# Last expert step of a mixture-of-experts layer: four experts of 32 slots side by side in place of two passes of 64 slots

## Chip, core and metric

One core of a Trainium2 chip runs the whole kernel. The metric is the device time of one execution in microseconds (us). The matrix engine, TensorE, is PE in the rows, with its weight loads as PEld; VectorE is DVE, ScalarE is ACT, GpSimd is POOL, and SyncE is SP, which issues nearly all transfers from the device's memory.

## The reference

Two layers, each on 256 tokens of 1024 values in float32. A layer is a token mixer (four kinds of attention, gated and summed), a layer norm, a mixture of 32 experts in 8 groups of 4 with two experts for each token, and a second layer norm. The experts, cut to what matters:

```python
scores = sigmoid(xt @ w_router)                      # 256 x 32
g_sel  = argmax(sum of the two best biased scores of each group)
local  = top_k(biased scores of that group, 2)[1]
e_idx  = g_sel * 4 + local
gate   = scores at e_idx, divided by their sum
# for each expert e and each of its tokens:
hid = silu(xb @ w1[e]) * (xb @ w3[e])                # 1024 -> 256
ys  = hid @ w2[e]                                    # 256 -> 1024
y[token] += ys * gate
```

## The kernel before

The program is one straight list of instructions for each engine; a planner orders those of VectorE, ScalarE, GpSimd and SyncE by program order and dependences, while the order of PE in the expert stage is written out by hand (`manual_schedule`). `issue_after(x)` holds an instruction back until x is issued. PE multiplies float32 in two recorded instructions per matmul; a pair of types, a rounded high part and a remainder in the one-pass type float32r, is used where weights are split (`split`, L406: ScalarE copies the high part, VectorE subtracts).

Experts are handled in pairs: pair p is experts p and p + 16, and shares 64 slots, the first expert's tokens ahead of the second's. An expert stage has eight steps, q = 0 to 7, of two pairs, so four experts. A step (from L1449):

- For s = 0 and 1 (experts p, then p + 16) `head` (L1321) multiplies the gathered tokens with w1 and w3: 8 pieces of the contraction times 2 tiles of 64 columns, 512 wide, the tiles at PSUM rows 0 and 64. `hidden` (L1331) makes silu times product on ScalarE and VectorE, with a mask that keeps the rows of this half.
- `combine` (L1404) adds the outputs of the step before to the accumulators, through the transposed one-hot matrix of `flip_key` (L1386).
- In even steps `gates_of` (L1375) brings the gates to the slots by one matmul for each token block.
- `flip` transposes the hidden tiles, and `tail` (L1350) multiplies with w2: 2 passes, 2 halves of the output, 2 pieces, 2 tiles. ScalarE evicts a half, VectorE makes its remainder.

Expert weights are 1 MB tiles, in an order of SBUF slots (`SLOTS`, 20 of them) that `release` walks on: a tile's transfer starts when PE has used up the tile 20 places earlier. Each step takes 12 tiles, eight of w1 and w3 (`load_head`), then four of w2 (`load_out`). SyncE has eight completion semaphores, so at most eight transfers are outstanding.

Ahead of the first step the router's scores are turned into one-hot rows, ranks (`prk`, L1228), keys (`key`, a token's slot in its pair) and counts (`cn`). The first gather (`gather_first`, L1310) needs `x1l`, a remainder made by three VectorE subtractions (`rest`, L1179). Behind them in VectorE's queue stand the counts and gates (L1264 to L1283) and then the first evictions of the gather (`gathered`, L1294: even pieces on VectorE, odd ones on ScalarE).

Behind the last step the number of tokens of the fullest pair is loaded into a register on every engine (L1483), and a branch (L1581) runs the overflow loop over all pairs if it is over 64. Ahead of the branch stand, for the next layer, its first weight loads (`ahead`), `norm2` (L1525: statistics of the accumulators, power, scaling into R) with NW3 matmuls that keep PE busy, and the first two splits of the next layer's first weight (`pieces`). The next layer begins with transposes of R (L435).

## Time and profile before

| | us |
|---|---|
| median of the runs | 1007.54 |
| lowest and highest of the runs | 1006.2, 1008.17 |
| the profiled execution, its own time | 1012.46 |
| its span, first to last instruction | 1010.5 |
| PE busy in the span | 977.2 |

The profiled execution is a single one and has its own time beside its span. The two expert stages lie at about 281 to 502 us and 778 to 999 us. A row of the timeline gives the start and duration of an instruction or of several merged ones (x count), its engine, source line and operation, what it writes and reads, and in brackets how long the engine stood idle before it and what ended that. A row of a window gives the stretch, its length, then busy time and count of each engine, the granted PE clock as a share of 2.4 GHz, the mean busy share of the 16 DMA engines and what they moved.

### The profile page before, as it was taken

The numbers are of one execution on the slowest core, as the hardware profiler recorded it, in microseconds if no ns is written. First come the engines' busy times: TensorE is split into PE (matmuls) and PEld (weight loads), VectorE is DVE, ScalarE is ACT, GpSimd is POOL, SyncE is SP. The second block draws the span as 40 slices with busy tenths as digits, with TensorE's granted clock in tenths as the row PEclk, the third lists the DMA queues.
The fourth block names the chain that finished last, engine by engine and source line by source line (L and its number), as shares of the span: only waits on it lengthen the run. The fifth ranks groups of instructions, "written<-read, shape, count | busy, mean of one in ns | idle before, by whom it ended". The sixth has DMA issues, their size and how long they took to land. (4 is left out here: it accounts for less than half of the span.)

```text
span 1010.5 us, 16677 instructions
## 1 busy us (share of the span) xinstructions
PE 977.2 (97%) x6391; PEld 693.2 (69%) x6391; DVE 494.8 (49%) x1166; ACT 404.3 (40%) x864; POOL 201.8 (20%) x190
## 2 busy tenths in 40 slices
PE   7999999999989999999999999999999999999995
PEld 7989999999953434343497999989998343433432
DVE  4766777667651122221377666685687222211114
ACT  4756665665421212111164766566553111111111
POOL 5440123022020313000045201141112012130001
PEclk9989999999999999999999999999999999999998
DMA  8785444579779999999895454544996799999982
GB/s 276 246 256 166 131 164 127 167 276 410 265 248 395 383 412 413 413 413 413 300 304 143 130 157 135 164 146 157 336 404 212 291 411 412 413 407 414 413 354 85
DMA packets 121434, 287.09 MB, mean 284 GB/s; under 512 B 10398, under 2 KB 73636, under 8 KB 113668
## 3 DMA queue, kind: packets, MB, share of 16 engines
q1 hardware_dynamic: 119940, 282.48, 76.0%
q0 software_dynamic: 1264, 3.41, 1.4%
q8 instruction: 52, 0.85, 0.3%
q14 instruction: 34, 0.28, 0.1%
q10 hardware_dynamic: 144, 0.07, 0.0%
HBM read 284.55 MB, written 1.38 MB: 283 GB/s over the span
## 5 line engine op out<-in xcount | busy, mean ns | idle before, releaser
L417 DVE TENSOR_TENSOR b<-w,b 128x512 fp32r<-128x512 f32 (+2 forms) x294 | 212.7, 739 | 103.3 <-ACT b L412 98.9
L412 ACT ACTIVATE b<-w 128x512 fp32r<-128x512 f32 (+2 forms) x294 | 179.9, 623 | 131.1 <-PE pj L452 106.5
L450 PE MATMUL pj<-big,b 128*128 128x256 f32 x736 | 215.3, 292 | 0.8 <-DVE a L537 0.5
L452 PE MATMUL pj<-big,b 128*128 128x256 f32 x736 | 210.2, 286 | 1.2 <-DVE b L417 1.2
L451 PE MATMUL pj<-big,b 128*128 128x256 f32 x736 | 210.0, 285 | 0.0
L450 PEld LDWEIGHTS pj<-big,b 128*128 128x128 f32 x736 | 142.9, 194 | 7.6 <-issue 4.6
L452 PEld LDWEIGHTS pj<-big,b 128*128 128x128 f32 x736 | 142.9, 194 | 1.7 <-DVE b L417 1.7
L451 PEld LDWEIGHTS pj<-big,b 128*128 128x128 f32 x736 | 143.2, 195 | 0.1
L1327 PE MATMUL h<-xw,a 128*64 128x512 f32 x496 | 127.6, 600 | 4.0 <-DVE a L1300 4.0
L1327 PE MATMUL h<-w,a 128*64 128x512 f32 x400 | 119.3, 593 | 0.0
L1338 DVE SCALAR_TENSOR_TENSOR th<-th,h 128x256 f32<-128x256 f32 x32 | 13.5, 420 | 184.6 <-ACT th L1337 184.6
L1327 PEld LDWEIGHTS h<-xw,a 128*64 128x64 f32 x496 | 44.1, 139 | 74.3 <-issue 67.8
L1337 ACT ACTIVATE th<-h 128x256 f32<-128x256 f32 x32 | 12.3, 384 | 203.5 <-PE h L1327 203.5
L1362 DVE SCALAR_TENSOR_TENSOR b<-y,gcol,b 128x512 fp32r<-128x512 f32 x30 | 22.5, 751 | 112.7 <-ACT b L1361 112.7
L1368 PE MATMUL y<-w,hT 128*64 128x512 f32 x256 | 71.5, 595 | 1.9 <-ACT hT L1347 1.9
L1327 PEld LDWEIGHTS h<-w,a 128*64 128x64 f32 x400 | 37.6, 137 | 44.9 <-issue 44.3
L1361 ACT ACTIVATE b<-y,gcol 128x512 fp32r<-128x512 f32 x30 | 20.6, 688 | 96.7 <-PE y L1368 96.7
L542 POOL TENSOR_TENSOR R<-R,a 128x512 f32<-128x512 f32 x20 | 35.3, 1778 | 111.8 <-DVE a L537 106.3
L450 PE MATMUL pj<-b,big 128*128 128x256 f32 x192 | 55.9, 291 | 1.5 <-ACT b L412 1.3
L452 PE MATMUL pj<-b,big 128*128 128x256 f32 x192 | 55.0, 287 | 0.1
L451 PE MATMUL pj<-b,big 128*128 128x256 f32 x192 | 54.6, 285 | 0.0
L341 POOL TENSOR_TENSOR rs<-ve,mhalf 128x1 f32<-128x1 f32 (+1 forms) x6 | 4.1, 680 | 221.2 <-DVE mr L1538 160.9
(367 smaller groups left out, 1739.4 us busy)
## 6 DMA issues: line engine op xcount, KB each, us to landing
xw<-in_moe_w SPq DMA_DIRECT2D x124, 512.0 KB, 10.2
w<-in_moe_w SPq DMA_DIRECT2D x100, 512.0 KB, 10.2
w<-in_w_gate SPq DMA_DIRECT2D x32, 1024.0 KB, 5.6
w<-in_moe_w SPq DMA_DIRECT2D x32, 1024.0 KB, 12.9
w<-in_w_in SPq DMA_DIRECT2D x18, 1024.0 KB, 10.7
xw<-in_moe_w SPq DMA_DIRECT2D x18, 1024.0 KB, 13.8
w<-in_w_out SPq DMA_DIRECT2D x8, 1024.0 KB, 5.2
ohl<-in_moe_w SPq DMA_DIRECT2D x12, 512.0 KB, 10.5
```

Of the source, the lines that this page charges most:

```text
L412: act.activation(h, v, AF.Copy)
L417: dve.tensor_sub(lo, v, h.bitcast(F32))
L450: pe.matmul(o, lh, rh, start=start, stop=False, skip_group_check=True)
L451: pe.matmul(o, lh, rl, start=False, stop=False, skip_group_check=True)
L452: return pe.matmul(o, ll, rh, start=False, stop=stop, skip_group_check=True).ins
L542: eng.tensor_tensor(merged[:, c:c + 2, :], merged[:, c:c + 2, :], tc_, op=OP.add)
L1327: pe.matmul(ph[64 * i:64 * i + 64], xs(j, i), a13[i][j], start=(j == 0), stop=(j == 7), skip_group_check=True)
L1337: act.activation(tv, h1, AF.Tanh, scale=0.5)
L1338: dve.scalar_tensor_tensor(tv, tv, 1.0, h1, op0=OP.add, op1=OP.mult)
L1361: act.activation(ys[:, 0, :], py, AF.Copy, scale=gcol)
L1362: dve.scalar_tensor_tensor(ys[:, 1, :], py, gcol, ys[:, 0, :].bitcast(F32), op0=OP.mult, op1=OP.subtract)
L1368: pe.matmul(pys[fh][64 * i:64 * i + 64, :], hTs[s][:, c, 64 * i:64 * i + 64], a2[s][i][c][:, fh * 512:fh * 512 + 512], start=(s == 0 and c ...
```

## The change

The last step (q = 7, `QUADS`) holds four experts at once, each with 32 slots of its own. `quad_keys` moves the keys of its four experts: the second expert of a pair gets slots 33 to 64, and a token whose rank is over 32 gets a key beyond the step. `prk` no longer counts the first expert ahead of the second for these pairs (`PAIRED`). `head4` runs one pass of 8 pieces times 4 tiles of 32 columns, `tail` one pass with 4 tiles of 32; there is one `hidden` and one `flip`. The loads of this step come first halves first. A count above 32 in this step sends the rest of these tokens to the overflow loop.

Beside it: the first gather's evictions alternate by pairs of pieces, and gates and counts come behind them; `gates_of` multiplies high part and remainder side by side in float32r and adds them on VectorE; the register loads come behind step 5; in layer 0 the next layer's first two splits come between the last two evictions, the statistics behind them, the branch ahead of the rest of `norm2`, and NW3 is 7 instead of 12. The overflow loop takes the new forms; small scratch arrays move into an existing tile.

```diff
+QUADS = (NQ - 1,)
-NW3 = 12
+NW3 = 7
+PAIRED = slice(2 if 0 in QUADS else 0, NP - 2 if NQ - 1 in QUADS else NP)
...
-                    h, lo = pieces[j] if j < len(pieces) else split(w[j // 4][:, j % 4, 0:n], n, after=xt_ins if j < 4 else None)
+                    h, lo = pieces[j] if j < len(pieces) else split(w[j // 4][:, j % 4, 0:n], n, after=(norm_ins[1] if l else xt_ins) if j < 4 else None)
...
-                    loads += [partial(load_head, q, s, h) for h in range(4)]
+                    if q not in QUADS:
+                        loads += [partial(load_head, q, s, h) for h in range(4)]
+                if q in QUADS:
+                    loads += [partial(load_head, q, s, h) for h0 in (0, 2) for h in (h0, h0 + 1) for s in range(2)]
...
-                pe.matmul(prk[:, :, NP:], oneb, osel[:, tb, None, 0:NP].to_broadcast([128, 2, NP]), start=False, stop=False,
-                          skip_group_check=True)
+                pe.matmul(prk[:, :, NP + PAIRED.start:NP + PAIRED.stop], oneb,
+                          osel[:, tb, None, PAIRED].to_broadcast([128, 2, PAIRED.stop - PAIRED.start]), start=False,
+                          stop=False, skip_group_check=True)
...
+            def quad_keys(q):
+                ps_ = slice(2 * q, 2 * q + 2)
+                kq = key.rearrange("p t (i e) -> p t i e", i=2)[:, :, :, ps_]
+                up = tB[:, 8 * q:8 * q + 8].rearrange("p (t i e) -> p t i e", t=2, i=2)
+                for i, most in enumerate((32.5, 0.5)):
+                    dve.tensor_scalar(up[:, :, i], kq[:, :, i], most, 32.0, op0=OP.is_gt, op1=OP.mult)
+                dve.tensor_add(kq, kq, up)
+                return dve.tensor_add(keyP[:, :, ps_], kq[:, :, 0], kq[:, :, 1]).ins
...
+            if NQ - 1 in QUADS:
+                with tc.issue_after(made):
+                    made = quad_keys(NQ - 1)
             with tc.issue_after(made):
                 for tb, js in ((0, JH[1]), (1, JH[0]), (1, JH[1])):
                     made = rest(dve, tb, js)
...
+            def gates_and_counts():
+                counted = dve.tensor_add(cs, cn[:, 0:NP], cn[:, NP:]).ins
+                with tc.issue_after(counted):
+                    for q in QUADS:
+                        cq = cs[:, 2 * q:2 * q + 2]
+                        dve.tensor_tensor(cq, cn[:, 2 * q:2 * q + 2], cn[:, NP + 2 * q:NP + 2 * q + 2], op=OP.max)
+                        dve.tensor_scalar(cq, cq, 32.0, None, op0=OP.add)
+                    ...
+                    dve.tensor_copy(grs[:, :, :, 0], grP)
+                    dve.tensor_sub(grs[:, :, :, 1], grP, grs[:, :, :, 0].bitcast(F32))
+                    dve.tensor_reduce(cmax, cs, axis=AX.X, op=OP.max)
+                    return dve.tensor_copy(cmi, cmax).ins
...
-                            gathered(xg, j - 1, pxs[j - 1])
-                            gathered(xg, j, pxs[j])
+                            done = [gathered(xg, k, pxs[k], j % 4 == 1) for k in (j - 1, j)][1]
+                return done.ins
...
+            def head4(xs, a13):
+                ph = op.tile([128, 2, 256], F32, name="h")
+                for j in range(8):
+                    for t in range(4):
+                        pe.matmul(ph[32 * t:32 * t + 32], xs(j, t), a13[t][j], start=(j == 0), stop=(j == 7),
+                                  skip_group_check=True, tile_position=(0, 32 * t))
+                return ph
...
-                            for i in range(2):
-                                pe.matmul(pys[fh][64 * i:64 * i + 64, :], hTs[s][:, c, 64 * i:64 * i + 64],
-                                          a2[s][i][c][:, fh * 512:fh * 512 + 512], start=(s == 0 and c == 0),
-                                          stop=(s == len(hTs) - 1 and c == 1), skip_group_check=True)
-                        if s == len(hTs) - 1:
-                            evac(fh)
+                            for r0, n, a2 in tiles:
+                                pe.matmul(pys[fh][r0:r0 + n, :], hT[:, c, r0:r0 + n], a2[c][:, fh * 512:fh * 512 + 512],
+                                          start=(s == 0 and c == 0), stop=(end and c == 1), skip_group_check=True,
+                                          tile_position=(0, r0) if n == 32 else None)
+                        if end:
+                            with tc.issue_after(between()) if fh and between else ExitStack():
+                                evac(fh)
...
-                gp = op.tile([128, 2], F32, name="y")
+                gp = op.tile([128, 2, 2], F32, name="y")
                 for tb in range(2):
-                    pe.matmul(gp, oh[:, tb, :].bitcast(F32), g[:, tb, :], start=(tb == 0), stop=(tb == 1))
+                    pe.matmul(gp, oh[:, tb, :], g[:, tb], start=(tb == 0), stop=(tb == 1))
...
-                    dve.tensor_copy(gcol[H], gp[H, i:i + 1])
+                    dve.tensor_reduce(gcol[H], gp[H, i], axis=AX.X, op=OP.add)
...
+            def next_pieces():
+                pieces.extend(split(ahead[0][0][:, i, :], 416, after=lows[-1]) for i in range(2))
+                return last_split[0]
...
+                    if q == 5:
+                        counts, (cnt_max,) = nc.values_load_multi_w_load_instructions(cmi[0:1, 0:1], min_val=0, max_val=S + 32)
...
+                    if final and l + 1 < layers:
+                        next_slots = list(mixer_slots(l + 1))
+                        ahead = [slot(next_slots[0])]
...
-            norm_ins = norm2(lastc)
+            with ExitStack() if last else tc.issue_after(last_split[1]):
+                stats()
             if not last:
-                pieces = [split(ahead[0][0][:, i, :], 416, after=norm_ins[i]) for i in range(2)]
-            with tc.If(cnt_max > W):
-                with tc.For_i(0, (cnt_max - 1) // W, 1):
-                    dve.tensor_scalar(key, key, float(-W), None, op0=OP.add)
-                    with tc.For_i(0, NP, 1) as pi:
-                        overflow(pi)
-                norm2()
+                with tc.If(cnt_max > W):
+                    rest_of_overflow()
+                norm_ins = norm2(lastc)
+            else:
+                norm2(lastc)
+                with tc.If(cnt_max > W):
+                    rest_of_overflow()
+                    norm2()
```

## Rows read from the trace of the kernel before

**Rows 1.** Page, busy time of each engine, share of the span, instructions.

```profile
PE 977.2 (97%) x6391; PEld 693.2 (69%) x6391; DVE 494.8 (49%) x1166; ACT 404.3 (40%) x864; POOL 201.8 (20%) x190
```

**Rows 2.** Windows over both expert stages; the last columns: PEclk, DMA share, GB/s.

```profile
293.00:468.00 175.00, 172.45 (x842) 73.42 (x840) 36.06 (x81) 27.33 (x56) 23.51 (x19) 0.99 1.02 403
793.00:968.00 175.00, 172.45 (x850) 73.02 (x847) 36.06 (x81) 27.33 (x56) 23.50 (x19) 1.00 1.02 409
```

**Rows 3.** Chain of waits, last steps, layer 1; the third: the timeline.

```profile
964.11 0.61 PE y L1379 x4
...
965.52 7.09 PE y L1368 x32
...
965.53 0.64 PE L1368 MATMUL y<-R,hT 128*64 128x512 f32 x1
...
972.61 13.73 PE h L1327 x64
...
986.34 2.05 PE acc L1412 x8
...
989.52 7.09 PE y L1368 x32
```

**Rows 4.** Timeline: last step of layer 0, then the first eviction in layer 1.

```profile
474.68 10.89 PE L1327 MATMUL h<-xw,a 128*64 128x512 f32 x49
...
491.75 7.09 PE L1368 MATMUL y<-w,hT 128*64 128x512 f32 x32 [0.31 <-ACT hT L1347]
...
497.17 0.69 ACT L1361 ACTIVATE b<-y,gcol 128x512 fp32r<-128x512 f32 x1 [5.20 <-PE y L1368]
...
994.94 0.69 ACT L1361 ACTIVATE b<-y,gcol 128x512 fp32r<-128x512 f32 x1 [5.20 <-PE y L1368]
```

**Rows 5.** Issue, landing: last tile and next weight (layer 0), last tile (layer 1).

```profile
L1015 SPq DMA_DIRECT2D w<-in_moe_w x1: 328/328/328, 473.2 to 473.2; - x1
DMA to landing us min/median/max: 15.1/15.1/15.1
...
L318 SPq DMA_DIRECT2D w<-in_w_in x1: 383/383/383, 474.5 to 474.5; - x1
DMA to landing us min/median/max: 16.0/16.0/16.0
...
L1015 SPq DMA_DIRECT2D w<-in_moe_w x1: 328/328/328, 969.1 to 969.1; - x1
DMA to landing us min/median/max: 14.9/14.9/14.9
```

**Rows 6.** Timeline at the stage start, layer 1; 290.61 is of layer 0.

```profile
290.61 0.33 SPq L1015 DMA_DIRECT2D xw<-in_moe_w  x1
...
777.56 0.19 DVE L1243 TENSOR_TENSOR keyP<-key 128x32 f32<-128x32 f32 x1
...
778.46 3.20 DVE L1180 TENSOR_TENSOR big<-X,big 128x512 fp32r<-128x512 f32 x3
...
782.45 1.72 DVE L1270 TENSOR_SCALAR gr<-gr,gsum 128x32 f32<-128x32 f32 x2
...
784.67 5.81 PE L1327 MATMUL h<-xw,a 128*64 128x512 f32 x18 [2.00 <-DVE a L1300]
...
790.05 0.33 SPq L1015 DMA_DIRECT2D xw<-in_moe_w  x1
```

**Rows 7.** Windows at the stage's start, with the granted clock (PEclk).

```profile
303.30:306.60 3.30, 3.30 (x10) 1.02 (x11) 0.51 (x2) 0.38 (x1) 0.00 (x0) 0.52 1.04 421
...
784.70:788.20 3.50, 3.50 (x10) 1.33 (x12) 1.38 (x4) 2.17 (x5) 0.00 (x0) 0.51 0.37 154
788.20:790.00 1.80, 1.80 (x12) 0.80 (x10) 0.00 (x0) 0.00 (x0) 0.00 (x0) 1.00 0.00 0
```

**Rows 8.** Timeline at the boundary of the layers: a split, the first transpose.

```profile
502.69 0.54 DVE L417 TENSOR_TENSOR b<-w,b 128x416 fp32r<-128x416 f32 x1
...
507.16 0.41 PE L435 MATMUL pj<-K,R 128*128 128x128 f32 x2 [0.30 <-PEq L1581]
```

More of the change, by code (lines that the diff above doesn't have):

```diff
@@ L1348, in flip, with pair_tiles, tail @@
                 return hT
-            def tail(hTs, a2, gcol, out, final=None):
+            lows = []
+            pieces = []
+            def pair_tiles(a2):
+                return [(0, 64, a2[0]), (64, 64, a2[1])]
+            def tail(passes, gcol, out, final=None, between=None):
                 pys = [op.tile([128, 512], F32, name="y") for _ in range(2)]
@@ L1452, in build @@
                     ths = []
-                    for s in range(2):
+                    if q in QUADS:
+                        a13q = [a13s.pop((q, s)) for s in range(2)]
+                        ph = head4(lambda j, t: xgs[b][:, j, o + 32 * t:o + 32 * t + 32],
+                                   [a13q[t % 2][t // 2] for t in range(4)])
+                        release(8)
+                        ths.append(hidden(ph, misc(6)))
+                    for s in range(2) if q not in QUADS else ():
                         ph = head(lambda j, i: xgs[b][:, j, o + 64 * i:o + 64 * i + 64], a13s.pop((q, s)))
                         release(3 if q == 1 and s == 0 else 4)
-                        ths.append(hidden(ph, mk[:, s, q:q + 1]))
+                        with ExitStack() as behind:
+                            for c_ in counts if q == 6 else ():
+                                behind.enter_context(tc.issue_after(getattr(c_, "ins", c_)))
+                            ths.append(hidden(ph, mk[:, s, q:q + 1]))
                     if o and more:
@@ L1510, in overflow @@
                 gather(xg, oh, 128)
-                gcol = gates_of(oh, gc)
+                gcol = gates_of(oh, gs2)
                 oht = flip_oh(oh)
@@ L1515, in overflow, with stats @@
                 yi = iter((y2[:, 0:2], y2[:, 2:4]))
-                ys = tail([flip(hidden(ph, misc(6)))], [a2], gcol, lambda dt: next(yi))
+                ys = tail([(flip(hidden(ph, misc(6))), pair_tiles(a2))], gcol, lambda dt: next(yi))
                 combine(ys, oht)
             if l + 1 < layers:
-                ahead = [slot(p) for p in mixer_slots(l + 1)]
+                ahead += [slot(p) for p in next_slots[1:]]
             last = l == layers - 1
-            def norm2(lastc=None):
-                st2 = sm("bst", 2, 4, 6)
+            st2 = sm("bst", 2, 2, 6)
+            def stats():
                 for n in range(2):
@@ L1529, in norm2, with rest_of_overflow @@
                         dve.bn_stats(st2[:, tb, n, :], acc[tb][n])
+            def rest_of_overflow():
+                with tc.For_i(0, (cnt_max - 1) // W, 1):
+                    dve.tensor_scalar(key, key, float(-W), None, op0=OP.add)
+                    with tc.For_i(0, NP, 1) as pi:
+                        overflow(pi)
+                stats()
+            def norm2(lastc=None):
                 mv = sm("bmv", 2, 2)
```

78 lines of the change are left out of this document (41 added, 37 removed).

## Prediction, made before the change was run

> **What bounds the kernel now.** I read the page first: TensorE (PE) is busy for 97% of the span [rows 1], so the question is what PE waits for once it has less to do. Second, windows over the two expert stages: there the DMA engines are as full as PE, share 1.02 at 403 and 409 GB/s [rows 2]. Third, the chain of waits through the last expert step of layer 1: one head of two passes (13.73 us), the combine of the step before (2.05 us), a short flip, and the tail (7.09 us), all PE [rows 3]. Fourth, the landings. The last expert tile is issued at 473.2 and lands 15.1 us later, at 488.3 (layer 0), and at 969.1 + 14.9 = 984.0 (layer 1) [rows 5], while the tail that reads it begins at 491.75 and 989.52 [rows 3, 4]. So PE ends each stage only 3.5 to 5.5 us behind a stream that is itself full. Whoever makes the last step shorter than that on PE meets the DMA. Last, the start of the stage: PE stands still for 2.00 us behind small VectorE work, and the stream restarts only when PE has used up the first head tiles [rows 6].
>
> **The last step, four abreast.** Instruction counts on PE stay (32 head and 16 tail matmuls per layer, each recorded as two); what changes is that four of 32 columns would share the array instead of two of 64. Today the two tiles of a pair run side by side: in the tail the first ones start at 965.52 and 965.53, and a pass of 16 head matmuls takes 6.87 us, half of 13.73 [rows 3]. No row has four abreast. Bounds: as fast as pairs are now, head 6.87 and tail 3.55 (half of 7.09), or no gain over pairs, 13.73 and 7.09. I take the first, because the pair, which starts together, is the nearest row, and keep the second as a rival. From the end of the head to the tail PE needs 989.52 - 986.34 = 3.18 us [rows 3], 3.0 with one transposed tile fewer. The second hidden stage on ScalarE and VectorE went on beside the combine and saves nothing.
>
> The page "TensorEngine Tiling (Array Packing)" of the Trainium skill, Theoretical Speedup, allows up to four times for 32 columns; "TensorE: Matmul & The Clock Gate", Part 3, gives 2.38 times for three such tiles. By the latter, an estimate, four would give 3.17 times one: head 8.7 us, tail 4.5 us, and the sum would be about 2 us smaller. No run here shows it yet.
>
> **The start of each stage.** Gates and counts (VectorE from 778.46 + 3.20 = 781.66 to 782.45 + 1.72 = 784.17, 2.5 us [rows 6]) leave the path between the last subtraction and the first evictions, and the first pair of evictions goes to ScalarE. The 2.00 us wait [rows 6] should vanish; PE then follows its own gather. Added ahead of the subtractions are four small VectorE operations that prepare the keys of the last step: 0.19 us each by the nearest row [rows 6], less where they overlap; 0.6 us for all, 0.3 to 0.8 at the bounds. Net 1.4 us earlier (1.2 to 1.7). The moved work (about 14 small operations, three new ones included) then lies beside a first pass of 6.87 us; only the gates two passes later and the next one-hot wait for it. The stream follows: first issues at 290.61 and 790.05 come when PE is done with the first tiles, and between 788.2 and 790.0 the DMA share is 0.00 [rows 6, 7]. In layer 1 the granted clock is at its lower level, 1.2 GHz, from 784.7 to 788.2 (0.51), right after the wait, which costs 3.5 x 0.49 = 1.7 us before that restart [rows 7]. Without the wait I take it as gone there. In layer 0 the same wait brought no fall at once; the one there, at 303.3 [rows 7], lies behind the restart and is hidden by the stream.
>
> **Gates in one pass.** Matmuls with two columns become half as many instructions with four columns in a one-pass type. They cost 0.61 us on the chain per even step [rows 3]; half is 0.3, and the transposed one-hot still holds the PSUM buffer. I take 1.0 us per layer over four steps (0.5 to 2.3), and count it at nothing, because it only adds to the wait for the last tile. Without that wait it would be worth 1.0 us per layer.
>
> **Where PE meets the stream.** Layer 0, in times of before: the tail could start at 474.68 - 1.4 - 1.0 + 6.87 + 3.0 = 482.2 [rows 3, 4]. Its fourth matmul needs the last tile, at 488.3 - 1.4 = 486.9. PE waits 4.7 us, part of it already in the head, whose last weights land some 10 us before the last tile (four tiles of 1.05 MB at 403 to 409 GB/s). Half a tail later, at 488.65, ScalarE evicts; before it did at 497.17 [rows 4]. Gain 8.5 us. The first two splits of the next layer are moved behind this eviction and ahead of the second: they need a weight that lands at 474.5 + 16.0 - 1.4 = 489.1 [rows 5], and ScalarE asks for it at 488.65 + 0.69 = 489.3. It is just there. The second eviction queues behind them on ScalarE and is ready when PE's fourth combine matmul is over: costed at nothing; if that weight were late by some us, so would be the boundary.
>
> Layer 1: 972.61 - 1.4 - 1.0 - 1.7 + 6.87 + 3.0 = 978.4, the last tile at 984.0 - 3.1 = 980.9; wait 2.5 us, first eviction at 982.65 instead of 994.94 [rows 3 to 5]. Gain 12.3 us, or 10.6 if the clock falls there again.
>
> **The boundary.** Today two splits of the next layer sit on VectorE between the statistics (one is the row at 502.69), and PE starts the transposes only behind the branch, at 507.16, 10.0 us after the first eviction of the step at 497.17 [rows 4, 8]. Two splits leave that path (2 x 0.54). The transposes no longer stand behind the branch (0.30, the wait that the row names) nor behind the second halves of the scaling, 128x512 on ScalarE like the 0.69 us evictions [rows 4, 8]. Against that the branch now lies ahead of the aggregation, where VectorE empties its queue (0.35 us, between 0 and twice the 0.30), and two later splits follow the scaling and delay the first transposed pieces (0.3). Net 1.1 + 0.3 + 0.7 - 0.35 - 0.3 = 1.4 us (0 to 2.0). The register loads move into step 5, on every engine: on PE behind a tail of 32 instructions that asks for nothing more, on SyncE among transfers that land 15 us after their issue [rows 3, 5]; nothing, 0.5 us per engine if it stood bare. Five clock-keeping matmuls fewer: nothing, they only fill the shorter gap. SyncE meets the branch with the next layer's loads outstanding, as now. The end of layer 1 keeps its order; nothing (-0.5 to 0.5).
>
> **What the waits cost.** Two new PE waits of 4.7 and 2.5 us stand right ahead of the tails. The only rows for that are ambiguous: 2.00 us of waiting was followed by a fall once and not the other time [rows 6, 7]. I deduct one fall out of two, 1.7 us. The page "TensorE: Matmul & The Clock Gate" of the Trainium skill, Part 1 (HAM oscillation), describes a kernel in which every wait for DMA between bursts brought the lower clock back; by that both tails would pay, 1.7 us less gain (c).
>
> **Sum.** 8.5 + 12.3 + 1.4 - 1.7 = 20.5 us. The profiled execution took 1012.46 us (span 1010.5 and 2.0 around it), so 992.0; the runs' median, 1007.54, is 4.9 lower, and the same difference from it gives 987.0.
>
> **Rivals.** (a) Four tiles run as two pairs. Then the last step is as long as now, no weight is late, and the gain is 1.4 + 1.0 + 0.2 per layer, 1.7 for the clock, 1.4 at the boundary: 8.3 us, 999.2. For it: no row shows four. Against: the pair's common start [rows 3]. (b) The stream is no limit: then PE's own gain counts, 6.87 + 3.55 + 0.2 + 1.4 + 1.0 = 13.0 per layer, plus 1.7 and 1.4: 29.1, 978.4. Against: the landings. (c) The landings don't follow the earlier start, and both tails run at the lower clock: 8.5 - 1.4 - 1.7, 12.3 - 3.1 - 1.7 and 1.4: 14.3, 993.2. (d) Four tiles lose a part to each other: midway to pairs, head and tail are 10.3 and 5.3 us; the waits hide the heads' 3.4 (all but 0.9 in layer 1), the tails' 1.8 each stay: 4.5 us less, 991.5. (e) Slower: 32-column tiles run one after another. Head 27.4, tail 14.2 us, 20.8 more per layer; less 2.6 per layer and 3.1: 33 us slower, 1040. It decides as soon as less than about 1.7 tiles run at a time. Against: pairs run together [rows 3]. (f) The change doesn't do what it says, because an expert of the last step has over 32 tokens and the overflow loop runs: 16 pairs of 6.3 MB at 409 GB/s are 246 us per layer, 1233 or more. The reference's routing of its own inputs gives 16, 10, 23, 23 tokens in layer 0 and 24, 16, 29, 26 in layer 1.
>
> **How the numbers follow.** Forecast 58%, (a) 9%, (b) 6%, (c) 9%, (d) 9%, (e) 4%, (f) 2%, something unseen that eats the gain 3%. The forecast's own range is 982 to 992. The range that holds 8 in 10 reaches from 978 to 997; outside lie (a), (e), (f) and the unseen case, 18%. Faster by over 0.2%, about what a measurement of this kernel can tell from no change, 0.90; within 0.2%, 0.03; slower 0.07.
>
> **What would show it.** Four h-matmuls of the last step starting within some 20 ns of each other and a head of about 7 us; the first weight load of q = 7's tail waiting for a DMA, not for ScalarE; no PE wait of 2 us ahead of the first head; transposes 8.6 us after the first eviction. Wrong: a head of 13.7 us (a) or 27 (e); no wait for weights (b); the last tile landing as far from PE's gather as now (c).

## The result, and the profile after

The changed kernel took 991.9 us (median; 990.08 to 995.11) beside 1007.86 us for the kernel before on the same chip: ratio 0.984, 95% interval 0.982 to 0.987, 16.0 us faster. The forecast was 987.0 us, in a range of 978 to 997, and a gain of 20.5. The profiled execution took 993.61 us (span 991.8). A second set of times, made later, gave 996.07 us (992.5 to 997.51) beside 1008.52, ratio 0.986 (0.983 to 0.990). The two medians of this kernel lie 4.2 us apart, those of the kernel before 0.7; the profiles don't settle why.

The page of after: busy time of each engine, and from the chain that ended last the shares by engine.

```profile
PE 948.9 (96%) x6345; PEld 675.3 (68%) x6345; DVE 495.9 (50%) x1178; ACT 403.2 (41%) x860; POOL 200.6 (20%) x190
...
PE 29%; DMA 14%; DVE 4%; issue 1%; ACT 1%; POOL 0%; SPq 0%; DVEq 0%; ACTq 0%; POOLq 0%
```

PE lost 28 us of work against [rows 1], and transfers are now 14% of the chain that ended last. Where they stand in it, the timeline of the last steps shows (start, duration, engine, line, operation, and in brackets the idle time before and what ended it):

```profile
476.27 0.61 PE L1365 MATMUL h<-xw,a 128*32 128x512 f32 x3
...
476.29 0.59 PE L1365 MATMUL h<-w,a 128*32 128x512 f32 x1
...
476.70 0.60 PE L1365 MATMUL h<-xw,a 128*32 128x512 f32 x3
...
485.26 3.62 PE L1414 MATMUL y<-w,hT 128*32 128x512 f32 x26 [1.51 <-DMA w<-in_moe_w]
...
487.20 0.69 ACT L1405 ACTIVATE b<-y,gcol 128x512 fp32r<-128x512 f32 x1 [4.62 <-PE y L1414]
...
974.03 3.62 PE L1414 MATMUL y<-w,hT 128*32 128x512 f32 x26 [1.21 <-DMA w<-in_moe_w]
...
975.97 0.69 ACT L1405 ACTIVATE b<-y,gcol 128x512 fp32r<-128x512 f32 x1 [4.26 <-PE y L1414]
```

The quartet is there: three matmuls of 32 columns start at 476.27, the fourth at 476.29, and the next four 0.43 us later. The head takes 7.0 us (472.38 to 479.38) instead of 13.73 [rows 3], and 26 of the tail's 32 instructions take 3.62 us, all 32 took 7.09; a tail without a wait takes 3.64 in all (below, the run with one tile fewer). And there is the new wait: the tail stops after six instructions for the last tile, 1.51 us in layer 0, 1.21 in layer 1. The first evictions stand at 487.20 and 975.97, before at 497.17 and 994.94 [rows 4]. Issue and landing of the last tile of layer 0, as in [rows 5]:

```profile
L1018 SPq DMA_DIRECT2D w<-in_moe_w x1: 328/328/328, 469.6 to 469.6; - x1
DMA to landing us min/median/max: 15.6/15.6/15.6
```

It lands at 469.65 + 15.6 = 485.2, and the tail goes on at 485.26; in layer 1 the last one lands at 974.0. So PE now ends each stage with the stream, as forecast. The boundary of the layers is another matter. Timeline behind the first eviction of 487.20, then a window (the last three columns are the granted clock PEclk, DMA share, GB/s):

```profile
492.59 0.28 DVE L1616 BATCH_NORM_AGGREGATE bmv<-bst 128x2 f32<-128x12 f32 x2
...
492.65 3.26 PE L306 MATMUL y<-K 128*128 128x256 f32 x14 [0.94 <-DVEq L1662]
...
497.27 0.37 SPq L321 DMA_DIRECT2D w<-in_w_uq  x1
...
497.36 0.15 DVE L901 TENSOR_SCALAR sg<-vcol 128x1 f32<-128x1 f32 x1 [4.49 <-SPq L1662]
...
497.44 0.16 DVE L1617 TENSOR_SCALAR ve<-bmv 128x2 f32<-128x2 f32 x1
...
500.72 0.69 PE L438 MATMUL pj<-K,R 128*128 128x128 f32 x2 [4.81 <-ACT R L1656]
```

```profile
500.70:504.20 3.50, 3.48 (x19) 3.48 (x20) 2.77 (x6) 2.47 (x6) 0.40 (x1) 0.57 1.00 259
```

The aggregation is done at 492.87. Then VectorE stands still for 4.49 us ahead of a one-column operation of the next layer, `sg` (L901), released by SyncE's queue at the end of the branch (L1662). Behind it in VectorE's queue stand `ve`, and so GpSimd's power (L344), the scaling and the transposes: PE waits 4.81 us. This wait is the stall in what follows. From the first eviction to the transposes it takes 13.5 us, before it took 10.0 [rows 4, 8], forecast were 8.6. The clock falls with the wait: 0.57 from 500.7 to 504.2. The clock-keeping matmuls (L306, seven now) end at 495.9; that there are five fewer was taken for nothing because the gap would be shorter, and it was longer. Whether twelve would have kept the clock up was not run.

What SyncE does there follows from its issues. This is the last of the next layer's first four weight loads:

```profile
L321 SPq DMA_DIRECT2D w<-in_w_in x1: 4902/4902/4902, 481.3 to 481.3; - x1
...
DMA to landing us min/median/max: 15.5/15.5/15.5
```

It was issued at 481.31 and landed 15.5 us later, at 496.8; the next issue stands at 497.27, 0.5 us behind that landing, though the branch is not taken. `sg` waits for the same thing: in the trace the waits ahead of it on VectorE are for the very eight signals that SyncE passes one after the other at the end of the branch, the last at 497.1. Why it waits for them is read from the kernel's text and not from the trace: the next layer's small tiles take over memory into which expert tiles were loaded (the pool `xw` is closed before the next layer's pool `at` is opened).

### The profile page after: what moved, and what is told of

The parts are those of the page before. It is cut to its first block, busy times and chain, and to the rows that moved or that the text cites. A ratio compares the mean times of both kernels' runs of the same rounds, so it can differ in the third digit from the quotient of the medians.

```text
span 991.8 us, 16594 instructions
## 1 busy us (share of the span) xinstructions
PE 948.9 (96%) x6345; PEld 675.3 (68%) x6345; DVE 495.9 (50%) x1178; ACT 403.2 (41%) x860; POOL 200.6 (20%) x190
## 5 line engine op out<-in xcount | busy, mean ns | idle before, releaser
L453 PEld LDWEIGHTS pj<-big,b 128*128 128x128 f32 x736 | 141.5, 192 | 6.8 <-issue 3.5
L455 PEld LDWEIGHTS pj<-big,b 128*128 128x128 f32 x736 | 141.5, 192 | 3.4 <-DVE b L420 3.4
L454 PEld LDWEIGHTS pj<-big,b 128*128 128x128 f32 x736 | 141.7, 193 | 0.1
L1356 PE MATMUL h<-w,a 128*64 128x512 f32 x384 | 112.1, 593 | 0.0
L1356 PE MATMUL h<-xw,a 128*64 128x512 f32 x384 | 98.0, 593 | 0.0
L1414 PE MATMUL y<-w,hT 128*64 128x512 f32 (+1 forms) x256 | 66.7, 595 | 5.0 <-DMA w<-in_moe_w 2.7
L1356 PEld LDWEIGHTS h<-xw,a 128*64 128x64 f32 x384 | 31.4, 137 | 53.7 <-issue 51.4
L1356 PEld LDWEIGHTS h<-w,a 128*64 128x64 f32 x384 | 35.4, 137 | 44.9 <-issue 44.0
L839 POOL TENSOR_SCALAR bias<-OH 128x384 f32<-128x384 f32 x16 | 21.5, 1345 | 120.2 <-DVE mn L560 113.5
## 6 DMA issues: line engine op xcount, KB each, us to landing
xw<-in_moe_w SPq DMA_DIRECT2D x124, 512.0 KB, 10.3
w<-in_moe_w SPq DMA_DIRECT2D x100, 512.0 KB, 10.6
w<-in_w_in SPq DMA_DIRECT2D x18, 1024.0 KB, 10.6
```

Of the source, the lines that this page charges most:

```text
L453: pe.matmul(o, lh, rh, start=start, stop=False, skip_group_check=True)
L454: pe.matmul(o, lh, rl, start=False, stop=False, skip_group_check=True)
L455: return pe.matmul(o, ll, rh, start=False, stop=stop, skip_group_check=True).ins
L839: pool.tensor_scalar(bs, mc["sw3"][:, 0:384], slope_sw[2 * hp + hh], None, op0=OP.mult)
L1356: pe.matmul(ph[64 * i:64 * i + 64], xs(j, i), a13[i][j], start=(j == 0), stop=(j == 7), skip_group_check=True)
L1414: pe.matmul(pys[fh][r0:r0 + n, :], hT[:, c, r0:r0 + n], a2[c][:, fh * 512:fh * 512 + 512], start=(s == 0 and c == 0), stop=(end and c == 1 ...
```

## Experiments

Times "after the keys" count from when VectorE is free for the operation that makes the keys (L1248, before L1241), 0.3 us ahead of its row. "Restart" is the first tile issued when PE has used up the first head tiles [rows 6].

**The two kernels once more.** The changed kernel:

> The changed kernel once more, for a second profiled execution. Theory 1 (the three subtractions at 4.8 us in layer 0 of its first profile were a chance of that execution, the wait of 4.5 us behind the branch is not): 3.2 to 3.5 us for the three, first head of layer 0 6.2 us after the keys instead of 7.75, and again some 4.5 us ahead of sg and 13 to 14 us from first eviction to transposes; median 990 to 994. Rival (the subtractions collide with GpSimd in this kernel every time): 4.8 us again.

```profile
282.33 3.19 DVE L1186 TENSOR_TENSOR big<-X,big 128x512 fp32r<-128x512 f32 x3
...
286.46 4.94 PE L1356 MATMUL h<-xw,a 128*64 128x512 f32 x22
...
497.31 0.15 DVE L901 TENSOR_SCALAR sg<-vcol 128x1 f32<-128x1 f32 x1 [4.38 <-SPq L1662]
```

The subtractions take 3.19 us, not the 4.78 of the first profile, and the head starts 6.15 us after the keys instead of 7.75; the wait ahead of `sg` is there again, 4.38 us, and 13.4 us from first eviction (487.25) to transposes (500.66). So the loss at the start of layer 0 was a chance of one execution; the stall came in both. Median 996.07, 2 us above the range that was expected for it. The kernel before:

> The kernel before once more, for a second profiled execution. Theory 1 (the falls of the clock at 300 to 308 us and at 784 us come from its 2.0 us PE waits at the start of each expert stage): falls at both places again, restart to last landing again 197 to 198 us in layer 0. Rival (the clock falls at other places in each execution): one or both are missing, and the stream of layer 0 then takes 194 us, as in layer 1.

```profile
287.04 6.16 PE L1327 MATMUL h<-xw,a 128*64 128x512 f32 x20 [2.00 <-DVE a L1300]
...
292.34 0.33 SPq L1015 DMA_DIRECT2D xw<-in_moe_w  x1
...
286.00:290.00 4.00, 2.96 (x8) 1.28 (x10) 2.44 (x7) 2.17 (x5) 0.35 (x1) 0.61 0.53 223
```

Here the clock fell in layer 0 right at the 2.00 us wait (0.61 from 286 to 290) and not at 303; in layer 1, where it fell in the first profile [rows 7], not at all. The last tile of layer 0 landed 193.6 us after the restart, not 197.7. The rival holds: the wait is in every execution, the fall is not, and its place changes.

**The stall alone.** `sg` is only put later in VectorE's queue:

```diff
-                dve.tensor_scalar(sg, vcol[:, 70 + l:71 + l], 1.0 - li, None, op0=OP.mult)
+                with tc.issue_after(norm_ins[1]) if l else ExitStack(): dve.tensor_scalar(sg, vcol[:, 70 + l:71 + l], 1.0 - li, None, op0=OP.mult)
```

> The changed kernel with one operation moved: the scaling factor of the next layer's fourth attention branch (sg, one column on VectorE) is issued behind the normalisation of the last block instead of wherever it falls (it fell right behind the branch). Theory 1 (the new wait at the layer boundary is sg, which waits for SyncE at the end of the branch and holds the aggregation's successor ve behind it on VectorE): the 4.49 us wait ahead of sg leaves the path, the way from the first eviction of layer 0's last step to the first transposes falls from 13.5 us to about 9.0, the rest stays; median about 987.4, 4.5 below the 991.9 of the changed kernel. Rival (SyncE itself is the stall: it issues the next layer's loads only after the branch, so weights are late in place of sg): the boundary shortens by less than 2 us and PE then waits for a DMA or for ScalarE's pieces; median 990 or more.

```profile
492.00 0.17 DVE L1617 TENSOR_SCALAR ve<-bmv 128x2 f32<-128x2 f32 x1
...
492.30 0.58 POOL L349 DMA_DIRECT2D a<-in_ln_g  x1 [72.55 <-DVE mr L1619]
...
492.90 0.75 POOL L344 TENSOR_TENSOR rs<-ve,mhalf 128x2 f32<-128x2 f32 x1
...
495.94 0.44 PE L438 MATMUL pj<-K,R 128*128 128x128 f32 x2 [0.94 <-ACT R L1656]
...
496.14 0.15 DVE L901 TENSOR_SCALAR sg<-vcol 128x1 f32<-128x1 f32 x1
```

Measured: 987.79 us (985.95 to 989.75), ratio to the kernel before 0.978 (0.976 to 0.981). `ve` follows at once, `sg` runs without a wait at 496.14, PE waits 0.94 us instead of 4.81, the transposes come 9.66 us behind the first eviction, and the clock stays at 1.00 there. SyncE still leaves the branch only at 495; nothing that PE needs waits for it. Theory 1 holds, the rival falls.

**The branch where it was.** `norm2` of layer 0 first, then the branch, `sg` as in the changed kernel:

```diff
+                norm_ins = norm2(lastc)
                 with tc.If(cnt_max > W):
                     rest_of_overflow()
-                norm_ins = norm2(lastc)
+                    norm2()
```

> The changed kernel with the overflow branch of layer 0 behind the normalisation again, as in the kernel before; all else as changed. Theory 1 (the wait is not the transfers that are outstanding, but what stands behind them in VectorE's queue): with the normalisation ahead of the branch, sg can hold nothing that the transposes need; from first eviction to transposes 9.5 to 10.0 us instead of 13.5; median 988 to 989. Rival (SyncE's wait for every outstanding transfer holds the layer boundary wherever the branch stands): 13 us again, PE waiting behind the branch until the last of those transfers has landed, and 991.5 to 992.

```profile
486.69 0.69 ACT L1405 ACTIVATE b<-y,gcol 128x512 fp32r<-128x512 f32 x1 [4.56 <-PE y L1414]
...
493.23 1.53 DVE L1655 TENSOR_SCALAR R<-acc,bmv,rs 128x512 f32<-128x512 f32 x2 [0.77 <-POOL rs L344]
...
495.46 0.41 PE L438 MATMUL pj<-K,R 128*128 128x128 f32 x2 [1.23 <-DVEq L1663]
```

Measured: 987.83 us (983.98 to 992.14), ratio 0.980 (0.975 to 0.984); 8.8 us from first eviction to transposes, less than the 9.5 to 10.0 expected. The wait needs both: the branch ahead of the normalisation and `sg` ahead of `ve`. PE waits 1.23 us for the branch, and still has the transposes sooner than with `sg` moved: the scaling starts 6.5 us behind the first eviction, not 7.4, which the next experiment explains.

**GpSimd's issues.** In the rows of the kernel with `sg` moved, GpSimd issues a load of gamma (L349, 0.58 us) between `ve` and the power. Moved behind `mr` (GpSimd's second product of the normalisation, which `norm2` now returns as `norm_ins[2]`), with `sg` moved as well; the main line of the edit:

```diff
-                load_gb(pool, gbx[c], 2, l - 1, c * 256, c * 256 + 256)
+                with tc.issue_after(norm_ins[2]): load_gb(pool, gbx[c], 2, l - 1, c * 256, c * 256 + 256)
```

> The kernel with sg behind the normalisation, and besides GpSimd's loads of gamma and beta for the next layer issued behind its part of the normalisation (the power that gives 1/deviation) instead of ahead of it. Theory 1 (the branch ahead of the normalisation let one 0.59 us issue slip in ahead of that power on GpSimd, on the path): the boundary falls from 9.65 to about 8.9 us, what remains above the forecast's 8.6 being the transposes that still wait for the second halves on ScalarE; median 0.7 below 987.8, 987.1, a difference that the times alone hardly tell. Rival (GpSimd is not on the path): 9.65 again.

```profile
494.17 0.72 POOL L344 TENSOR_TENSOR rs<-ve,mhalf 128x2 f32<-128x2 f32 x1 [74.04 <-DVE mr L1619]
...
495.57 0.63 POOL L349 DMA_DIRECT2D a<-in_ln_g  x1 [0.41 <-issue]
...
497.03 0.41 PE L438 MATMUL pj<-K,R 128*128 128x128 f32 x2
```

The power follows `ve` at once and the transposes come 8.83 us behind the first eviction: theory 1, now 0.2 above the forecast's 8.6. The median, 987.46 (986.12 to 990.03), ratio 0.978 (0.976 to 0.981), does not tell it from 987.79, as expected.

**The four abreast alone.** `QUADS = ()`: the last step in pairs, all other moves kept.

> The changed kernel with the last step in pairs again (two passes of 64 slots, no tokens doubled), every other move kept. Theory 1 (nearly all of the gain is the four abreast, and the other moves are worth little because the boundary gave theirs back): head 13.7 and tail 7.1 us again, first evictions of the last step 8.8 us later in layer 0 and 9.1 in layer 1; part of the 4.5 us wait behind the branch is then covered by the longer step; median 1005 to 1010, about the kernel before. Rival (the forecast's sum: start, gates, clock and boundary carry 8.3 us by themselves): 999 to 1001.

The chain of waits through the last step of layer 1 (start, us, what):

```profile
961.68 13.73 PE h L1356 x64
...
978.58 7.09 PE y L1414 x32
```

Measured: 1001.82 us (1001.21 to 1003.0), ratio 0.993 (0.990 to 0.995), between the two expectations (the forecast's rival (a) had 999.2). Head and tail are as in [rows 3]. But the first evictions come 213.4 us after the keys in both layers, against 206.3 and 205.7 with four abreast: 7.1 and 7.8 us, less than the 8.8 and 9.1 that I took; 0.5 us of that is that in pairs no time goes to the new keys (head 0.5 us sooner), the rest is not accounted for. The stall is hidden, since the step ends later than SyncE's transfers (9.66 us from first eviction to transposes). Between two kernels without the stall, this one and the one with `sg` moved, four abreast are worth 14.0 us; the other moves 7.0.

**The stream as the limit.** One w2 tile of step 5 is not loaded; its neighbour's stands in for it, so this kernel leaves out one expert's w2 in each layer and serves for times alone.

```diff
+                if (q, s, i) == (5, 1, 1):
+                    a2s[q, s][i] = a2s[q, s][0]
+                    return
```

> The changed kernel without one of the w2 loads (1.05 MB) of step 5 in each layer; that expert pair computes with its neighbour's weights instead. Theory 1 (the stream sets the end of the last step): the last expert tile lands 2.6 us earlier in each layer, the waits ahead of the tails (1.51 and 1.21 us) go to zero, the first evictions come 1.5 and 1.2 us earlier, and what waits for the branch in layer 0 ends up to 2.6 us earlier: 3 to 4 us off the whole, 988 to 989. Rival (PE or the release of buffers sets it, and the stream has room): the first evictions stay within 0.5 us, 991.5 to 992.

```profile
482.96 3.62 PE L1417 MATMUL y<-w,hT 128*32 128x512 f32 x26 [0.26 <-DMA w<-in_moe_w]
...
498.04 0.69 PE L438 MATMUL pj<-K,R 128*128 128x128 f32 x2 [4.42 <-ACT R L1659]
...
970.93 3.64 PE L1417 MATMUL y<-w,hT 128*32 128x512 f32 x32 [0.53 <-ACT hT L1388]
```

Measured: 988.47 us (988.23 to 990.67), ratio 0.979 (0.976 to 0.982), 3.4 below the changed kernel's first median and 7.6 below its second. The wait ahead of the tail is 0.26 us in layer 0 and none in layer 1, restart to last landing 193.2 and 191.8 us (1.3 and 2.4 less than in the first profile of after, not 2.6 in both), and the stall behind the branch stays (4.42). Theory 1 holds; in layer 1 no wait for a tile is left, so there PE would be the limit again. The other way round, with more of PE's time taken away, the first step four abreast too (in the kernel with `sg` and GpSimd's loads moved):

```diff
-QUADS = (NQ - 1,)
+QUADS = (0, NQ - 1)
```

> The kernel with sg and GpSimd's loads mended, with the first expert step four abreast as well (QUADS holds step 0 and the last one; on these inputs no expert of step 0 has more than 32 tokens). Theory 1 (the stream sets the time between restart and last landing, so PE's shorter steps are worth nothing where a full stream lies behind them): step 0 takes 10 us less on PE per layer, and the last landing comes 193 to 195 us after the restart as ever; the keys of step 0 are prepared ahead of the one-hot, 0.5 us later start; median 987 to 989. Rival (PE's time counts in every step): 10 us less per layer, 968 to 970.

```profile
465.23 1.06 PE L1365 MATMUL h<-xw,a 128*32 128x512 f32 x6
...
468.05 3.63 PE L1365 MATMUL h<-xw,a 128*32 128x512 f32 x28 [1.76 <-DMA xw<-in_moe_w]
...
478.87 0.59 PE L1365 MATMUL h<-w,a 128*32 128x512 f32 x1 [2.10 <-DMA w<-in_moe_w]
...
479.90:483.30 3.40, 3.40 (x20) 0.89 (x10) 0.00 (x0) 0.00 (x0) 0.00 (x0) 0.51 1.01 425
...
488.72 3.62 PE L1414 MATMUL y<-w,hT 128*32 128x512 f32 x26 [0.33 <-DMA w<-in_moe_w]
```

Measured: 993.06 us (992.53 to 996.27), ratio 0.985 (0.983 to 0.987), 5.6 us slower than without. PE reaches the last step of layer 0 at 465.23, 6.7 us sooner than in the kernel it was built on, and gives it back at once: 1.76, 1.49, 1.54 and 2.10 us of waiting for tiles inside one head. Behind the last of these the clock fell (the window's 0.51), and so it did in layer 1, behind 2.39 us. The last landing is 195.1 and 193.9 us after the restart, as ever. And the restart itself comes 3.8 and 2.2 us later after the keys than in the kernel it was built on (whose layer 1 had the collision described below as well): the keys of step 0 stand ahead of the one-hot, in both layers the subtractions met GpSimd (below), and the clock fell behind that wait. The direction of theory 1 holds, its 987 to 989 does not: I costed only the keys.

**The start of the stage.** Gates and counts back between the last subtraction and the first evictions, which still begin on ScalarE:

```diff
-                with tc.issue_after(gather_first(xgs[0], ohs[0], acc[0] + acc[1])):
-                    routed = gates_and_counts()
+                gather_first(xgs[0], ohs[0], acc[0] + acc[1])
...
+            with tc.issue_after(made):
+                routed = gates_and_counts()
```

> The changed kernel with gates and counts back between the last subtraction and the first evictions at the start of each expert stage (the first evictions still begin on ScalarE). Theory 1 (the forecast's 1.4 us per layer, and the stream follows): first heads 7.3 to 7.8 us after the keys instead of 6.2, the stream's restart and the last landing 1.3 to 1.6 us later in both layers, more where the clock falls in the wait; 3 to 5 us slower than changed, 995 to 997. Rival (the stream hides the start): landings within 0.5 us of the changed kernel, 992.

```profile
285.76 1.94 PE L1358 MATMUL h<-xw,a 128*64 128x512 f32 x8
...
288.23 3.22 PE L1358 MATMUL h<-xw,a 128*64 128x512 f32 x14 [0.53 <-DVE a L1331]
```

Measured: 994.31 us (990.9 to 996.25), ratio 0.985 (0.981 to 0.989): not to be told from the changed kernel's two medians. In layer 0 the head starts 6.14 us after the keys all the same, because ScalarE evicts the first two pieces; the wait comes one pair later (0.53 us for VectorE, at 288.23), and the restart is at 10.57 instead of 9.82. So theory 1 falls in its size: of the 1.5 us that the restart gained (11.35 to 9.82), the gates' move is 0.75. The rest, 0.8, is net: ScalarE's turn brings about 1.3, and the new keys take back 0.5 (the run in pairs, without them, restarts at 9.32). Layer 1 says nothing here, a collision with GpSimd stood in it.

**That collision.** Timeline of the first profile of after, layer 0:

```profile
281.27 4.78 DVE L1186 TENSOR_TENSOR big<-X,big 128x512 fp32r<-128x512 f32 x3
...
282.59 2.60 POOL L1474 TENSOR_TENSOR x<-big,big 128x512 f32<-128x512 f32 x1
...
286.11 0.74 PE L1344 MATMUL acc<-OH,big 128*128 128x256 f32 x4 [1.89 <-DVE big L1186]
```

GpSimd's addition (L1474) runs from 282.59 to 285.19, and the three subtractions take 4.78 us: two took 1.1 us, the third 2.74, ending 0.9 us behind the addition. PE waits 1.89 us for it. In the kernel before the masks lasted until 284.2 in this layer, the subtractions ([rows 6] show those of layer 1) were done at 283.9, and the addition came behind them, at 284.32. The addition held back:

```diff
+                    if tb == fh == 0:
+                        pool.tensor_copy(t[:, 0:1], x1l[:, 1, 7, 127:128].bitcast(F32))
                     pool.tensor_tensor(t.rearrange("t (p j) -> t p j", j=8), *xv, op=OP.add)
```

> The changed kernel with one tiny GpSimd copy added ahead of the first residual half of each expert stage, which reads the last of the three VectorE subtractions, so that GpSimd begins its 128x512 addition only when they are done. Theory 1 (in layer 0 the subtractions were slowed by GpSimd's addition, 4.78 us for three against 3.20): they take 3.2 us again, PE's third gather pass and the first head start 1.4 to 1.6 us earlier in layer 0, the stream restarts as much earlier, and the first eviction of the last step follows; layer 1, where the two did not meet, stays; median 1.5 below the changed kernel, 990.4. Rival (the subtractions are slow for another reason, or another wait stands right behind): 4.8 us again or the head starts at the same time; 991.9.

```profile
281.01 2.64 POOL L1314 TENSOR_SCALAR mk<-th,K 64x8 f32<-64x8 f32 x4 [4.82 <-ACT th L1245]
...
282.38 3.22 DVE L1186 TENSOR_TENSOR big<-X,big 128x512 fp32r<-128x512 f32 x3
...
286.00 1.98 POOL L1476 TENSOR_TENSOR x<-big,big 128x512 f32<-128x512 f32 x1
```

Measured: 994.17 us (989.73 to 995.62), ratio 0.984 (0.981 to 0.987), and not the 990.4 expected: no gain in the median, which fits a collision that is not in every execution. Its mechanism shows in the traces: where GpSimd's four masks took 1.7 to 2.6 us in all, the addition slipped in ahead of the third subtraction, which then took 2.7 us (5 of 18 stage starts of kernels with the new keys and a free addition); where the last mask took 2.0 us by itself, it did not (13 of 18). Here the masks were quick too (2.64) and the three subtractions took 3.22, because the addition came at 286.00.

The page "SBUF — State Buffer" of the Trainium skill, section "Who interferes with whom", says that a VectorE operation with two inputs in SBUF contends with a GpSimd operation that reads SBUF, that the ports they share are an exclusive lock, and that the order of issue decides which of the two is blocked. The rows agree: 2.74 us instead of 1.1 for the subtraction behind the addition, ended 0.9 us behind it, and 2.60 us for that addition, begun during the second subtraction, where one that begins behind all three takes 1.93 (kernel before) or 1.98.

**Gates in two columns again.** `gates_of` with the float32 type and two columns, as before:

> The changed kernel with the gates in two columns and a two-pass type again. Theory 1 (the step of the forecast that counted them at nothing): PE's two gate matmuls take 0.6 instead of 0.3 us in each even step, no tail of the last step begins later, the wait ahead of it only gets shorter, and first eviction minus keys stays at 206 us within 0.4 in both layers. Rival (the saved time is on the path): first evictions 0.5 to 1.0 us later.

The eight gate matmuls of an even step took 1.26 us in a row instead of two lots of 0.38. In layer 0 the first eviction of the last step came 206.2 us after the keys, as in the other kernels whose layer 0 had neither the collision nor a fall of the clock (206.3 to 206.9): hidden, theory 1. In layer 1 the clock fell at 792, behind the restart:

```profile
792.00:796.00 4.00, 4.00 (x12) 1.12 (x10) 0.03 (x1) 0.20 (x1) 0.00 (x0) 0.57 1.01 414
```

There the last landing came 198.8 us after the restart instead of 193 to 195, so layer 1 (and the 997.5 us of this execution) says nothing on the gates. It says something on the clock, see below.

**All three mendings.** `sg`, GpSimd's loads and the held addition together:

> All three mendings in one kernel: sg behind the normalisation, GpSimd's gamma and beta loads behind its power, and GpSimd's first residual addition held until VectorE's last subtraction is done. Theory 1 (the stall behind the branch is worth 4 us, the issue on GpSimd 0.8, and the collision 1.6 us in some 3 of 18 stage starts, 0.3 us per run on the mean): no third subtraction over 1.2 us in either layer, first eviction to transposes 8.8 us, PE's first head 6.2 us after the keys in both layers; median 987, within 1 us of the two kernels with sg moved, and 4 to 6 below the changed kernel. Rival (the changed kernel's spread hides these): 990 or more.

```profile
280.07 2.60 POOL L1314 TENSOR_SCALAR mk<-th,K 64x8 f32<-64x8 f32 x4 [4.79 <-ACT th L1245]
...
281.44 3.16 DVE L1186 TENSOR_TENSOR big<-X,big 128x512 fp32r<-128x512 f32 x3
```

Measured: 987.25 us (985.85 to 989.42), ratio 0.979 (0.977 to 0.982). 8.83 us from first eviction to transposes, subtractions 3.16 us in both layers, although the masks were quick in both (2.60 us, as in the collision of the first profile of after), head 6.12 us after the keys in both. The three mended kernels (987.25, 987.46, 987.79) can't be told apart, and each is below the 991.9 and 996.07 of the changed one.

## Why the prediction came out as it did

The gain by stretches of the trace, for the two pairs of profiles (in us; each from differences of row times):

| stretch | forecast | first pair | second pair |
|---|---|---|---|
| to the first eviction of layer 0's last step | 8.5 | 10.0 | 10.0 |
| from there to the transposes | 1.4 | -3.5 | -3.4 |
| mixer of layer 1, to the keys | 0 | 0.6 | -2.2 |
| keys to the first eviction in layer 1 | 12.3 | 11.9 | 9.7 |
| end | 0 | -0.2 | -0.2 |
| deducted for the clock in the tails | -1.7 | 0 | 0 |
| sum | 20.5 | 18.7 | 13.9 |

The sums are differences of single executions' spans; the medians differ by 16.0 and 12.5 us, and the first profiled execution of the kernel before lay 4.6 us above its median. The 10.0 in both pairs is not the same 10.0: after the keys layer 0 gained 10.0 us in the first pair, with the collision in it, and 10.9 in the second, where the keys came 1.0 us later. The mixer's row holds clock falls on either side: in the kernel before at 552 to 560 us (0.57 in the first profile, 0.64 to 0.93 in the second), in the changed one behind the stall (until 504.2 in the first, until some 506 in the second).

That the time fell within the range is in part luck: in the first pair the boundary missed by 4.9 us, and 1.5 us in layer 0, 1.7 that the tails did not pay and 0.6 in the mixer made up for most of it. Rival (d), whose head of 10.3 us is nowhere in the trace, gave 991.5, nearer to the first median than the forecast.

- **Four abreast at full rate: right.** Head 7.0 us, tail 3.62, forecast 6.87 and 3.55; rivals (a), (d) and (e) fall. Quartets follow each other in 0.43 us, and the pairs of the run with `QUADS = ()` do so too (one pass of 16 matmuls in 6.87 us, [rows 3]): twice the work in the same time.
- **PE meets the stream: right, and it limits both layers.** The wait for the last tile stands where forecast, the landings follow the restart (rival (c) falls, though its 993.2 is nearer to both medians than 987.0), and the two runs that took away bytes and PE's work show it from both sides. Rival (b) falls.
- **Layer 0, mis-sized: 10.0 instead of 8.5.** I took the landing of 488.3 for a property of the kernel. It held a clock fall at 303 [rows 7] that I had called "hidden by the stream". It wasn't: restart to last landing is 197.7 there and 198.8 where the clock fell at 792, and 192.8 to 195.1 in all the other layers of full-stream profiles. In the first pair the stream was 3.2 us shorter and the restart 1.5 us later than forecast (the collision), so the last tile landed at 485.2, 1.7 us ahead of the 486.9 forecast. From the tail's start to the last landing the forecast had 4.7 us; it was 2.6 (482.63 to 485.2), of which PE stood idle 1.51 (in layer 1 2.5 forecast, 2.2 measured, 1.21 idle).
- **The boundary: wrong.** Two steps failed, and two smaller ones beside them. "SyncE meets the branch with the next layer's loads outstanding, as now": before, nothing that PE needed stood behind SyncE's end of the branch; now `sg` did, ahead of `ve`. And the branch "where VectorE empties its queue (0.35 us)" asked what the branch itself costs and not which other instructions the planner would put behind it: `sg` on VectorE (4.5 us), a load's issue on GpSimd (0.8 us). With both mended the stretch is 8.8 us, 0.2 from the forecast's 8.6. The step on "the second halves of the scaling" is not borne out either: with `sg` moved, the first transpose waits 0.94 us for ScalarE's scaling of both halves. Nor is "Five clock-keeping matmuls fewer: nothing, they only fill the shorter gap": the gap grew, and 4.81 us of it stayed empty.
- **The clock in the tails: mis-sized.** Of 20 tails that waited for a tile (0.26 to 1.51 us) the clock fell in 2, not in one out of two; both are among the 11 that waited 1.2 us or more. It fell where I hadn't looked: with the 4.4 to 5.1 us wait at the boundary, in 5 of 5 profiles that had it, and in none of the 7 without. From first eviction to transposes these five took 13.1 to 13.8 us, six of the seven 8.8 to 9.7 (the seventh, with 1.6 us ahead of `sg`, 10.6). The mixer behind it took 269.2 to 271.1 us up to the keys, in the seven 267.9 to 271.0, 1.5 less on the mean, although in three of those the clock fell at 541 to 543 us. Together that is some 5 us for the stall and the clock behind it; the medians 991.9 and 996.07 lie 4.1 and 8.3 above 987.8.
- **The start of the stage: right in size** (restart 9.8 instead of 11.35 us after the keys, 1.5; forecast 1.4), wrong in its parts: the gates' move is half of it, the other half is what ScalarE's turn leaves over the new keys. The collision with GpSimd, which takes it back in some executions, I did not see, though four new operations on VectorE are in the diff. In layer 1 the 1.7 us for the clock came out in the first pair and not in the second, where the kernel before had no fall there.
- **Gates at nothing: right**, by the run with two columns. Their size, 1.0 us per layer, came out by luck: the 0.61 us read from [rows 3] is half of the group, which takes 1.26 us; with four columns it is two lots of 0.38 with a wait of 0.27 between them (for the transposed one-hot), and an even step's path is 0.23 us shorter, 0.9 per layer.

The page "TensorE: Matmul & The Clock Gate" of the Trainium skill, Part 3, gives 2.38 times for three tiles of 32 columns; the estimate worked out from it was 8.7 us for the head. It took 7.0, and four tiles kept the pace of two, so the measurement decides against it here. Its Part 1 (HAM oscillation) describes waits for transfers that bring the lower clock back each time; the waits of up to 1.51 us ahead of the tails did so in 2 of 20, the wait of 4.4 to 5.1 us at the boundary in 5 of 5.

## What to carry to other kernels

When a branch or any wait is moved ahead, list for each engine what the planner may now issue behind it, and for each such instruction whose memory it takes over: one column that nobody needs soon can hold a queue that everybody needs. A length read from one execution holds that execution's chances; ask for the same length in the other layer, and where the two differ (197.7 and 194.0 us here) find out why before either goes into a sum. Shortening the engine that runs beside a full stream pays only in the stretch behind the last landing, and ahead of the restart.

## What the runs showed of the hardware

- SyncE left a branch that wasn't taken only when its outstanding transfers had landed: in the first profile of after it had issued all that stands ahead of the branch by 486.2, the last of it landed at 496.8, and its next issue stood at 497.27. In eleven profiles of the changed kernel and its variants SyncE passed the signal of that last landing 0.01 to 0.02 us behind it.
- A 128x512 subtraction on VectorE took 1.1 us alone and 2.7 us where a GpSimd addition of 128x512 had started first; the addition took 1.9 to 2.0 us alone and 2.6 to 2.7 where it began during a subtraction.
- A lower clock of 3 to 4 us shortly behind the restart went with a stream some 4 us longer, with the DMA share at 1.0, in the two cases seen (197.7 and 198.8 us). Counted issue by issue against the other layer of the same execution, both streams are 1.7 us behind from the sixteenth issue on, some 20 us after the restart and right behind the fall; that issue waits for PE's tail. They are 3.3 to 4.8 us behind some 110 us after the restart and don't catch up. So the first 1.7 us are tiles that PE freed later; where the rest comes from is not settled.
- Where the clock falls was not the same from execution to execution of one kernel; of nine stage starts with a wait of 1.9 to 2.0 us it fell at once in five.
